# A dilated-attention merge on one Trainium2 core: weighting the other two groups' values on VectorE for all pairs of heads

## The chip, the cores and the metric

The kernel runs on one core of one Trainium2 chip (trn2). The metric is device time in microseconds; the number that counts is the median of several executions. The engines are named as in the profile: PE (TensorE, with PEld for its weight loads), DVE (VectorE), ACT (ScalarE), POOL (GpSimd), and SP, which only issues transfers. Each works through its own queue of instructions in order.

## What is computed

Two layers of an encoder, 1024 tokens of width 1024. Layer 0 mixes tokens by latent attention, layer 1 by dilated windows; each ends with a squared-ReLU MLP. The change lies in layer 1. There, 16 heads of width 64 attend in three groups of windows (window 128, 512, 2048 with dilation 1, 4, 16), and the three outputs of a head are merged by the softmax of their log denominators:

```python
DIL_GROUPS = ((128, 1), (512, 4), (2048, 16))
for gi, (window, dilation) in enumerate(DIL_GROUPS):
    q = rms_norm(proj[:, :, gi, 0], g_q[gi])
    k = rms_norm(proj[:, :, gi, 1], g_k[gi])
    o, lse = dilated_group(q, k, proj[:, :, gi, 2], pos, table, window, dilation)
...
wts = jax.nn.softmax(jnp.stack(lses, axis=0), axis=0)
o = jnp.einsum('gbsh,gbshd->bshd', wts, o_all)
y = o.reshape(B, S, DIL_HEADS * DIL_HEAD_DIM) @ w_o
```

## The kernel before

`dil` runs the three groups one after the other. In a group it goes over eight pairs of heads (`pr` 0 to 7), and a pair takes four steps (`tp` 0 to 3) of two 128-token tiles each. Work of one step is spread over several rounds of the loop, so that at any time PE has the projection of one step, the scores of the step before and the output of an earlier one.

The way of one step, with the lines by which the profile names it:

- PE projects q and k into PSUM (`psproj`, L425 to L427: most of PE's time). ACT squares (`dsq`, L1850), DVE sums (`dms`, L1851), ACT and DVE make the reciprocal root (L112 to L116), DVE scales (`qn`, L1855), POOL applies the gain (`qn`, L1857).
- PE transposes (`psq`, L1866). ACT copies the high part of the result (`kT`, L1870) and DVE writes the low part, `psq` less that copy (`kT`, L1871). PE then makes the scores (`pss`, L1891).
- DVE adds the bias and takes the maximum (`pd`, L1907), ACT exponentiates (`pd`, L1913) and rounds (`ph`, L1950), POOL subtracts (`ph`, L1951), SP starts the transposing transfer (`pT`, L1952). PE multiplies by the values (`psav`, L1964 and L1965), and DVE adds the parts into `U` (L1966).

Beside this DVE and ACT split the weights of the next pair (`wqkl` and `wqkh`, L122 and L121), and in even pairs the values of coming pairs, two tiles at a time (`vr` on DVE, L1838; `vs` on ACT and POOL, L1837, L1839, L1840).

In groups 0 and 1 `finish` writes `U` of a pair to HBM. In the third group it merges: `um` loads the two other groups' values of the same pair from HBM, issued on ACT's queue a round before, in two halves of four tiles (128 x 4 x 2 x 128 f32); `factors` makes the weights `mgf` (L2019 to L2025); `merge` multiplies `U` and the two loaded planes by their weights (L2035) and adds them (L2037). The multiplications of the loaded planes are on POOL for pairs 0 to 6 and on DVE for the last; those of `U` and the additions are on DVE. After it `emit` transposes `U` on PE (`psot`, L2054). So an even pair's merge meets the value splits on DVE and POOL and an odd pair's doesn't.

The last pair's steps run beside the first output projection (`psy`), for which DVE splits the weights `wol`. This stretch, from the merge of pair 6 on, is called the tail here.

PE's order in `dil` is pinned as written. The orders of the other engines are set by the scheduler at build time from its own costs: an instruction that moves from one engine to another shifts its neighbours too.

Of the kernel before, what the change touches and what calls it, by code (L numbers as in the profile page):

```python
# [15 lines left out]
ALU = mybir.AluOpType  # L16
# [4 lines left out]
P = 128  # L21
# [20 lines left out]
class K:  # L42
# [1717 lines left out]
    def dil(self, at0, at1, tail, wqk, vd):  # L1760


        nc, a, tc = self.nc, self.a, self.tc
# [212 lines left out]
        def finish(u):  # L1976
# [25 lines left out]
            if pr < 7:  # L2002
                f = factors(pr, 0, 8)
                for hf in range(2):
                    merge(u, hf, f[:, :, 4 * hf : 4 * hf + 4])
                merged.append((u, u["at"], (0, 1)))
            else:
                last(u, 1)
# [19 lines left out]
        def merge(u, hf, f):  # L2028
            U = u["U"][:, 4 * hf : 4 * hf + 4, :]
            x = u["um"][hf]  # L2030
            heads = lambda y: y.rearrange("p t (h e) -> p t h e", h=2)
            for k, y in ((2, U), (1, x[:, :, 1]), (0, x[:, :, 0])):
                y4 = heads(y)
                eng = nc.gpsimd if k < 2 and u["pr"] < 7 else nc.vector
                eng.tensor_tensor(y4, y4, f[:, k].unsqueeze(3).broadcast_to([P, 4, 2, 64]), op=ALU.mult)  # L2035
                if k < 2:
                    nc.vector.tensor_tensor(U, U, y, op=ALU.add)  # L2037

        def last(u, hf):

            merge(u, hf, factors(u["pr"], 4 * hf, 4))
            merged.append((u, u["at"], (hf,)))
# [97 lines left out]
        for n, step in enumerate(steps):  # L2140
# [11 lines left out]
            if step is not None:  # L2152
                kind, g, pr, tp = step
# [4 lines left out]
                u = units[(g, pr)]  # L2158
# [229 lines left out]
```

## Time and profile before

| | us |
|---|---|
| median of 3 runs (3236.93 to 3240.54) | 3239.43 |
| the profiled execution | 3241.06 |
| its span in the trace | 3239.3 |
| POOL, multiplications of the loaded planes (L2035), 28 | 35.1 |
| POOL, all instructions, from 2283 to 2497 | 112.3 |
| DVE, all instructions, from 2283 to 2497 | 179.1 |
| PE, all matmuls, from 2283 to 2497 | 205.3 |

Positions are microseconds from the start of the span. The third group's merges begin at 2286, 2320, 2353, 2387, 2421, 2456 and 2492 (pairs 0 to 6); the tail then reaches to about 2560. A row of the timeline has start, length, engine, line, operation, output and inputs, and in brackets how long the engine was idle before it and what ended that. A row of groups has the count, the sum of busy time, the mean in ns, and the idle time before. Rows of one instruction can overlap by a tenth of a microsecond or so, since the next starts while the last drains.

### The profile page before, as it was taken

What the parts mean: (1) busy time and instruction counts of PE and PEld (TensorE: products, weight loads), DVE (VectorE), ACT (ScalarE), POOL (GpSimd) and SP (SyncE); (2) the same over time, 40 slices, a digit from 0 to 9 for tenths busy, and PEclk for the clock granted to TensorE, in tenths of its full rate; (3) what the DMA queues carried; (4) which work ended last, traced back from release to release, by engine and by line L of the source; (5) the groups of instructions that cost most, each with busy time, mean ns of one, the idle gap of its engine ahead of it and who ended that gap; (6) DMA issues with size and microseconds to landing.
All of it is one profiled execution on the core that took longest, in us unless ns stands there. A gap on an engine that the chain in (4) does not pass through costs nothing. (4 is left out here: it accounts for less than half of the span.)

```text
span 3239.3 us, 50775 instructions
## 1 busy us (share of the span) xinstructions
PE 3129.4 (97%) x18034; PEld 2646.8 (82%) x18034; DVE 2380.9 (74%) x4243; ACT 1733.1 (54%) x3507; POOL 920.0 (28%) x1226
## 2 busy tenths in 40 slices
PE   6989999999999999989999999998998999999999
PEld 6877677778788788767889998998998788888887
DVE  5677778746977776688757777777788588778566
ACT  5547777754544443542226676667565264544332
POOL 7454556530111100001124444444454002110010
PEclk9999999999999999999999999999999999999999
DMA  5352322253555779544638877887777636448664
GB/s 192 121 186 82 98 94 92 63 173 111 180 199 172 269 217 316 169 150 166 227 120 180 184 172 177 192 193 159 175 166 195 180 105 209 151 151 315 202 191 128
DMA packets 538927, 552.32 MB, mean 171 GB/s; under 512 B 199429, under 2 KB 421042, under 8 KB 538666
## 3 DMA queue, kind: packets, MB, share of 16 engines
q1 hardware_dynamic: 483978, 434.61, 47.3%
q0 software_dynamic: 27360, 91.31, 7.6%
q10 hardware_dynamic: 27328, 23.07, 2.7%
q8 instruction: 144, 2.36, 0.3%
q14 instruction: 117, 0.96, 0.1%
HBM read 376.17 MB, written 132.62 MB: 157 GB/s over the span
## 5 line engine op out<-in xcount | busy, mean ns | idle before, releaser
L426 PE MATMUL psm<-dl,dh 128*128 128x512 f32 x896 | 351.0, 392 | 8.6 <-DVE dl L122 8.5
L425 PE MATMUL psm<-hf,wf 128*128 128x512 f32 x896 | 349.5, 390 | 2.6 <-ACT wf L121 2.6
L427 PE MATMUL psm<-dh,dl 128*128 128x512 f32 x896 | 350.3, 391 | 0.0
L426 PE MATMUL psm<-hf,wf 128*128 128x512 f32 x896 | 348.6, 389 | 0.0
L427 PE MATMUL psm<-hf,wf 128*128 128x512 f32 x896 | 346.6, 389 | 0.4 <-DVE wf L122 0.4
L425 PE MATMUL psm<-dh,dh 128*128 128x512 f32 x896 | 335.0, 391 | 4.0 <-ACT dh L121 4.0
L425 PE MATMUL psproj<-wqkh,hTp 128*128 128x256 f32 x1024 | 301.6, 295 | 0.0
L427 PE MATMUL psproj<-wqkh,hTp 128*128 128x256 f32 x1024 | 290.1, 283 | 0.0
L426 PE MATMUL psproj<-wqkl,hTp 128*128 128x256 f32 x1024 | 289.9, 283 | 0.1
L121 ACT ACTIVATE dh<-ufr 128x1024 fp32r<-128x1024 f32 x112 | 118.3, 1057 | 175.0 <-PE psm L427 49.7
L426 PEld LDWEIGHTS psm<-dl,dh 128*128 128x128 f32 x896 | 169.2, 189 | 46.3 <-DVE dl L122 11.3
L425 PEld LDWEIGHTS psproj<-wqkh,hTp 128*128 128x128 f32 x1024 | 196.3, 192 | 8.5 <-issue 0.4
L425 PEld LDWEIGHTS psm<-dh,dh 128*128 128x128 f32 x896 | 168.4, 188 | 41.0 <-ACT dh L121 6.3
L425 PEld LDWEIGHTS psm<-hf,wf 128*128 128x128 f32 x896 | 168.2, 188 | 40.0 <-ACT wf L121 5.5
L427 PEld LDWEIGHTS psm<-dh,dl 128*128 128x128 f32 x896 | 169.1, 189 | 35.2
L427 PEld LDWEIGHTS psm<-hf,wf 128*128 128x128 f32 x896 | 168.2, 188 | 35.9 <-DVE wf L122 1.2
L426 PEld LDWEIGHTS psproj<-wqkl,hTp 128*128 128x128 f32 x1024 | 196.5, 192 | 0.3 <-DVE wqkl L122 0.3
L426 PEld LDWEIGHTS psm<-hf,wf 128*128 128x128 f32 x896 | 168.2, 188 | 34.7
L427 PEld LDWEIGHTS psproj<-wqkh,hTp 128*128 128x128 f32 x1024 | 196.2, 192 | 0.3 <-DVE hTp L2126 0.2
L122 DVE TENSOR_TENSOR dl<-ufr,dh 128x1024 fp32r<-128x1024 f32 x112 | 136.6, 1220 | 76.8 <-ACT dh L121 58.0
L756 DVE TENSOR_REDUCE mx<-pmx 128x1 f32<-128x512 f32 x256 | 165.1, 682 | 28.2 <-PE pmx L754 28.0
L122 POOL TENSOR_TENSOR pl<-p,ph 128x1024 fp32r<-128x1024 f32 x58 | 141.4, 2439 | 138.4 <-ACT ph L121 128.2
(400 smaller groups left out, 8926.4 us busy)
## 6 DMA issues: line engine op xcount, KB each, us to landing
ufr<-uf SPq DMA_DIRECT2D x112, 512.0 KB
adaw<-in_ada_w SPq DMA_DIRECT2D x96, 512.0 KB
w2r<-in_mlp_w SPq DMA_DIRECT2D x96, 512.0 KB
w1r<-in_mlp_w SPq DMA_DIRECT2D x64, 512.0 KB
bt<-bias SPq DMA_DIRECT2D x128, 256.0 KB
qkv<-st SPq DMA_DIRECT2D x32, 512.0 KB
hraw<-qkv SPq DMA_DIRECT2D x32, 512.0 KB
uf<-ub POOLq DMA_DIRECT2D x32, 512.0 KB, 3.8
```

Source lines behind the costliest of these rows:

```text
L121: nc.scalar.activation(hi, src, AF.Copy)
L122: (lo_eng or nc.vector).tensor_tensor(lo, src, hi.bitcast(F32), op=ALU.subtract)
L425: mm(out, lh, rh, start=first, stop=False)
L426: mm(out, lh, rl, start=False, stop=False)
L427: mm(out, ll, rh, start=False, stop=last)
L756: nc.vector.tensor_reduce(maxes[h][:, 2 * j + b : 2 * j + b + 1], ps, op=ALU.max, axis=AX.X)
```

## The change

The multiplications of the two loaded planes go to DVE for every pair. The two for the last pair were there already; 28 of them move, four for each of pairs 0 to 6. Nothing else is edited, and the same numbers are computed.

```diff
             for k, y in ((2, U), (1, x[:, :, 1]), (0, x[:, :, 0])):
                 y4 = heads(y)
-                eng = nc.gpsimd if k < 2 and u["pr"] < 7 else nc.vector
-                eng.tensor_tensor(y4, y4, f[:, k].unsqueeze(3).broadcast_to([P, 4, 2, 64]), op=ALU.mult)
+                nc.vector.tensor_tensor(y4, y4, f[:, k].unsqueeze(3).broadcast_to([P, 4, 2, 64]), op=ALU.mult)
                 if k < 2:
                     nc.vector.tensor_tensor(U, U, y, op=ALU.add)
```

Lines behind it move up by one: L2035 becomes L2034, L2037 becomes L2036.

The first place is DVE's queue at the merge of pair 2, which begins at 2353.33 in the profile. `U_30939` is that pair's output, `um_31807` and `um_31810` the loaded planes of its two halves, `mgf` the weights.

```order
-L2035 TENSOR_TENSOR U_30939<-U_30939,mgf_32018 128x512
+L2034 TENSOR_TENSOR U_30939<-U_30939,mgf_32018 128x512
+L2034 TENSOR_TENSOR um_31807<-um_31807,mgf_32018 128x4x128 x2
+L2034 TENSOR_TENSOR um_31810<-um_31810,mgf_32018 128x4x128 x2
 L1966 TENSOR_REDUCE U_30939<-psav_31869 128x128
+L2036 TENSOR_TENSOR U_30939<-U_30939,um_31807 128x512
 L1966 TENSOR_REDUCE U_30939<-psav_31875 128x128
 L1851 TENSOR_REDUCE dms_31882<-dsq_31881 128x8
-L2037 TENSOR_TENSOR U_30939<-U_30939,um_31807 128x512
```

All four multiplications stand together at the head of the merge, the second half's too, before the sums of `psav` and the `dms` of the running step; in POOL's queue the four rows are gone from behind `vs` (L1840).

The second place is the same queue some fifteen instructions on, in the same round. `wqkl` are the low parts of the next pair's weights.

```order
-L122 TENSOR_TENSOR wqkl_31903<-wqkr_31757,wqkh_31902 128x1024
 L116 SCALAR_TENSOR_TENSOR dry_31885<-drt_31887,dry_31885 128x8
-L122 TENSOR_TENSOR wqkl_31907<-wqkr_31760,wqkh_31906 128x1024
 L1855 TENSOR_TENSOR qn_31893<-psproj_31813,dry_31885 128x512
 L1838 TENSOR_TENSOR vr_31897<-vraw_31489,vs_31896 128x512
+L122 TENSOR_TENSOR wqkl_31903<-wqkr_31757,wqkh_31902 128x1024
 L1871 TENSOR_TENSOR kT_31495<-psq_31973,kT_31495 128x2x256
 L1966 TENSOR_REDUCE U_30939<-psav_32004 128x128
+L122 TENSOR_TENSOR wqkl_31907<-wqkr_31760,wqkh_31906 128x1024
 L1966 TENSOR_REDUCE U_30939<-psav_32010 128x128
```

One of the two weight splits now stands behind `kT` (L1871) instead of ahead of it, and `qn` is ahead of both.

The third place is DVE's queue in the tail, from the first addition of pair 6's first half on (`U_33179`).

```order
+L2036 TENSOR_TENSOR U_33179<-U_33179,um_34033 128x512
+L122 TENSOR_TENSOR wol_34238<-wor_34235,woh_34237 128x1024
+L1871 TENSOR_TENSOR kT_33729<-psq_34192,kT_33729 128x2x256
 L114 SCALAR_TENSOR_TENSOR drt_34117<-dms_34112,dry_34115 128x8
-L2037 TENSOR_TENSOR U_33179<-U_33179,um_34033 128x512
-L115 SCALAR_TENSOR_TENSOR drt_34117<-drt_34117,dry_34115 128x8
-L122 TENSOR_TENSOR wol_34238<-wor_34235,woh_34237 128x1024
-L116 SCALAR_TENSOR_TENSOR dry_34115<-drt_34117,dry_34115 128x8
-L1871 TENSOR_TENSOR kT_33729<-psq_34192,kT_33729 128x2x256
-L1855 TENSOR_TENSOR qn_34123<-psproj_34039,dry_34115 128x512
+L2036 TENSOR_TENSOR U_33179<-U_33179,um_34033 128x512
 L1966 TENSOR_REDUCE U_33179<-psav_34241 128x128
```

Here `qn` (L1855), L115 and L116 fall behind the sums of `psav` (L1966), and the second weight split and `kT` come earlier in the sequence; the four multiplications of pair 6 stand further ahead, behind its multiplication of `U`.

PE's order in the stretch of the merges stays as it was; in the tail a few matmuls, and in the second MLP more of them and the splits that feed them, change places.

## The prediction

> **What bounds the kernel now.** I read the page's engine row first, then busy time by stage, then what PE waited for in the stage of the change, then the single waits.
>
> ```profile
> PE 3129.4 (97%) x18034; PEld 2646.8 (82%) x18034; DVE 2380.9 (74%) x4243; ACT 1733.1 (54%) x3507; POOL 920.0 (28%) x1226
> core 0: us, PE busy (x) PEld busy (x) DVE busy (x) ACT busy (x) POOL busy (x), PEclk, DMA share, GB/s
> 2283.00:2497.00 214.00, 205.28 (x1867) 196.18 (x1866) 179.11 (x503) 130.26 (x437) 112.31 (x127) 1.00 0.74 171
> 2497.00:2560.00 63.00, 53.95 (x300) 43.12 (x299) 40.70 (x103) 20.76 (x64) 2.73 (x4) 0.97 0.64 188
> ...
> PE pss L1891 <- DVE kT L1871: 4.7, 4, 1.7
> PE psav L1964 <- DMA pT<-ph: 4.0, 5, 1.5
> ...
> 2364.41 0.86 PE L1891 MATMUL pss<-kT 64*128 64x256 f32 x10 [1.58 <-DVE kT L1871]
> 2389.69 0.26 PE L1964 MATMUL psav<-vs,pT 128*128 128x192 bf16 x1 [1.47 <-DMA pT<-ph]
> 2504.46 1.65 PE L1891 MATMUL pss<-kT 64*128 64x256 f32 x12 [4.85 <-DVE U L1966]
> ```
>
> PE is the bound: 97% of the span, and 205.3 of 214 us in the stretch of the seven merges. What a change off PE can do is lengthen or shorten PE's waits, and these are few: 4.7 us for DVE's `kT`, 4.0 us for transposing transfers, then 4.85 us at the start of the tail for DVE's sums. DVE is the second engine there, 179.1 of 214 us (84%), and it gets the work. POOL, which loses it, has 112.3 and stands first in none of PE's waits.
>
> **What moves, and its price.**
>
> ```profile
> L2035 POOL TENSOR_TENSOR um<-um,mgf 128x512 f32<-128x512 f32 x28 | 35.1, 1283 | 2.4 <-PE psav L1965 2.4
> ...
> L2035 DVE TENSOR_TENSOR um<-um,mgf x4: 684/688/691, 2511.9 to 2540.7; 128x512 f32<-128x512 f32 x4
> ...
> 2511.87 1.29 DVE L2035 TENSOR_TENSOR um<-um,mgf 128x512 f32<-128x512 f32 x2
> ```
>
> POOL loses 28 multiplications, 35.1 us. The same instruction stands on DVE already for the last pair, at 0.688 us; two in a row take 1.29, so each further one takes 0.61. DVE gets 28 x 0.61 = 17.1 us, 2.44 us at each merge. Taken alone that raises DVE to 196 of 214 us.
>
> Against it stands what POOL's multiplications cost DVE. Means in the stretch, and below them least, middle and greatest length:
>
> ```profile
> L2037 DVE TENSOR_TENSOR U<-U,um 128x512 f32<-128x512 f32 x24 | 20.5, 854 | 0.3
> L2035 DVE TENSOR_TENSOR U<-U,mgf 128x512 f32<-128x512 f32 x12 | 14.6, 1213 | 0.0
> L114 DVE SCALAR_TENSOR_TENSOR drt<-dms,dry 128x8 f32<-128x8 f32 x24 | 6.4, 265 | 0.1
> ...
> L2037 DVE TENSOR_TENSOR U<-U,um x32: 681/692/1360, 2289.3 to 2548.4; 128x512 f32<-128x512 f32 x32
> L2035 DVE TENSOR_TENSOR U<-U,mgf x16: 677/952/1714, 2286.2 to 2546.9; 128x512 f32<-128x512 f32 x16
> L114 DVE SCALAR_TENSOR_TENSOR drt<-dms,dry x24: 153/161/1005, 2291.7 to 2486.7; 128x8 f32<-128x8 f32 x24
> ```
>
> DVE instructions that read two SBUF tensors are at times two or six times as long as they need. The additions lose 24 x (0.854 - 0.69) = 3.9 us, L114 24 x (0.265 - 0.16) = 2.5, the multiplications of `U` 12 x (1.213 - 0.68) = 6.4. Not all of it goes away, as the even merge shows; about 10 us should, so DVE's net gain of work is some 7 us.
>
> **An even merge (pair 2).** The walk is along DVE:
>
> ```profile
> 2353.33 1.16 POOL L1840 TENSOR_TENSOR vs<-vr,vs 128x512 bf16<-128x512 f32 x1
> 2353.33 1.71 DVE L2035 TENSOR_TENSOR U<-U,mgf 128x512 f32<-128x512 f32 x1
> 2354.45 5.40 POOL L2035 TENSOR_TENSOR um<-um,mgf 128x512 f32<-128x512 f32 x4
> 2356.49 1.00 DVE L2037 TENSOR_TENSOR U<-U,um 128x512 f32<-128x512 f32 x1
> 2358.87 1.00 DVE L114 SCALAR_TENSOR_TENSOR drt<-dms,dry 128x8 f32<-128x8 f32 x1
> 2360.01 1.23 DVE L122 TENSOR_TENSOR wqkl<-wqkr,wqkh 128x1024 fp32r<-128x1024 f32 x1
> 2361.33 1.23 DVE L122 TENSOR_TENSOR wqkl<-wqkr,wqkh 128x1024 fp32r<-128x1024 f32 x1
> 2362.47 0.68 DVE L1855 TENSOR_TENSOR qn<-psproj,dry 128x512 f32<-128x512 f32 x1
> 2363.67 0.68 DVE L1871 TENSOR_TENSOR kT<-psq,kT 128x512 fp32r<-128x512 f32 x1
> 2372.39 0.69 DVE L1851 TENSOR_REDUCE dms<-dsq 128x8 f32<-128x512 f32 x1 [0.72 <-ACT dsq L1850]
> 2379.87 0.69 DVE L1871 TENSOR_TENSOR kT<-psq,kT 128x512 fp32r<-128x512 f32 x1 [2.03 <-ACT kT L1870]
> ...
> 2380.86 0.98 PE L1891 MATMUL pss<-kT 64*128 64x256 f32 x12
> ```
>
> `U`'s multiplication begins with POOL's L1840 and ends 0.6 us after that does: L1840 held it up, and stays, so its 1.71 us stay. L114 ends when POOL's fourth multiplication does (2359.85); it gets 0.84 us shorter, the first addition 0.31. Net: 2.44 - 0.84 - 0.31 = +1.29 us. In the new order one `wqkl` (1.14 us to the next start) falls behind `kT`, so the first `kT`, for which PE waits 1.58 us, comes only 1.29 - 1.14 = 0.15 us later. But that work comes back before the next `kT`: DVE has no gap from 2353.33 until the 0.72 us before 2372.39, and goes into that step 1.29 us late. One step on, `kT` ends at 2380.56, 0.30 us before PE uses it, and ACT, which sets that one, itself hangs on DVE's earlier L1907. Bounds are 0.15 us (the gaps swallow the rest) and 1.29 us; because of the 0.30 us I take the whole, 1.3 us for each of pairs 0, 2 and 4: 3.9 us. The additions queued behind the multiplications feed `psot` a step later, which has time.
>
> **An odd merge (pair 3).**
>
> ```profile
> 2387.02 1.51 DVE L2035 TENSOR_TENSOR U<-U,mgf 128x512 f32<-128x512 f32 x1
> 2388.62 1.36 DVE L2037 TENSOR_TENSOR U<-U,um 128x512 f32<-128x512 f32 x1
> 2396.70 0.69 DVE L1871 TENSOR_TENSOR kT<-psq,kT 128x512 fp32r<-128x512 f32 x1 [0.16 <-ACT kT L1870]
> ...
> 2398.20 0.98 PE L1891 MATMUL pss<-kT 64*128 64x256 f32 x12
> ```
>
> Here POOL's own first multiplication held `U` (1.51 to 0.68) and its second the addition (1.36 to 0.69): net 2.44 - 0.83 - 0.67 = +0.94 us, against 0.81 us between the end of `kT` and PE's use. The 1.47 us wait for `pT` is a transfer's and stays. Between 0 and 0.94 I take 0.3 us for each of pairs 1, 3 and 5: 0.9 us.
>
> **The tail (pair 6).**
>
> ```profile
> 2495.38 2.08 DVE L122 TENSOR_TENSOR wol<-wor,woh 128x1024 fp32r<-128x1024 f32 x1 [2.72 <-ACT woh L121]
> 2497.38 0.68 DVE L2035 TENSOR_TENSOR U<-U,mgf 128x512 f32<-128x512 f32 x1
> 2503.30 1.01 DVE L1966 TENSOR_REDUCE U<-psav 128x128 f32<-128x384 f32 x2
> ```
>
> PE's 4.85 us end with these sums, whose PSUM banks it needs. Ahead of them now stand 2.44 us more; `wol` loses 0.85 us of POOL's hold (2.08 to 1.23); `qn` (0.60) and about 0.2 us of small ones fall behind. Net +0.8 us at PE's wait. What falls behind is late next: `qn`, and L1907 by four multiplications less 0.85, so the last transposes. Bounds 0.8 and 2.44; I take 2.0.
>
> **New waits.** The multiplications wait for `um`'s loads; on DVE the sums, `dms` and L1907 are queued behind them. POOL's multiplications waited once, and not for a load:
>
> ```profile
> POOL um L2035 <- PE psav L1965: 2.4, 1, 2.4
> ```
>
> They started with or just after `U`'s multiplication, as they will now. I cost this at nothing. So too the shuffled order in the MLP, where DVE and ACT run ahead of a PE that is always full; without that cover it is a wait of the size of those above.
>
> **Sum:** 3.9 + 0.9 + 2.0 = 6.8 us. 3241.06 + 6.8 = 3247.9 for an execution like the profiled one; the median of the runs is 1.6 us below that one, so 3246.2. I say 3246, 0.2% more than 3239.43, and 0.2% (6.5 us) is also about what a measurement of this kernel can tell from no change.
>
> **Rivals.**
>
> *Covered.* DVE's gaps swallow all but the lower bounds: 3 x 0.15 + 0.8 = 1.3 us, hence 3240.7. For it: DVE is idle 16% of the stretch, and the gaps of 0.72 and 2.03 us. Against: none lies within 18 us of an even merge's start.
>
> *Freed.* It gets faster: POOL's hold was what made DVE late at `kT`, and the scheduler's shift of a `wqkl` behind it ends those waits. Place: the four waits for `kT`, 4.7 us, and with `wol` shorter up to 2.5 of the tail's 4.85. Price -7.2 us, 3232.2. It decides if DVE loses more than 2.44 us of held time per merge; the rows give 1.15 to 1.5. [...]
>
> *Unrelieved.* Other POOL work slides into the freed time and holds DVE as before, the new multiplications included: the gross 17.1 us reach PE, 3256.5. For it: L1840 and L1951 have two inputs and stand next in POOL's queue. It decides if `L2034` on DVE runs well over 0.7 us.
>
> *Clock.* PEclk is 1.00 in the stretch of merges, where no PE wait passes 1.7 us, and 0.97 over the 63 us with the 4.85 us wait: 1.9 us lost. If even merges' waits grew that long, three would cost 3 x (3 + 1.9) = 15 us: 3254. [...]
>
> **How the numbers follow.** Forecast 0.44 (its own range 3242 to 3252, two thirds of it beyond 0.2%: 0.29), covered 0.14, freed 0.20 (0.14 of it beyond 0.2%), unrelieved 0.17, clock 0.05. Slower: 0.29 + 0.17 + 0.05 = 0.51. Faster 0.14, within 0.2% 0.35. The range runs from 3232, where freed ends, to 3257, the gross price; outside are the far ends of three cases.
>
> **What would show it.** DVE in the same stretch about 7 us busier than 179.1 and L114 near 0.16 us show the relief; PE's wait for `kT` grown from 4.7 to about 8 us, in even pairs, the forecast; the tail's first wait about 5.6 us, the third term. A `kT` wait that falls speaks for freed, `L2034` on `um` over 0.9 us for unrelieved. PE waiting for `um`'s sums, or DVE idle ahead of `um`, would make the free terms wrong.

## The result, and the profile after

The changed kernel takes 3251.16 us, the median of 7 runs (3248.64 to 3253.80), beside 3239.43 us for seven runs of the kernel before: the ratio is 1.0035, with a 95% interval from 1.0025 to 1.0044. That is 11.7 us slower. Run again later, the pair gave 3253.50 against 3240.11 us (ratio 1.0042, 1.0030 to 1.0054).

The profiled execution of the changed kernel took 3253.80 us. Its page's engine row, with busy time, share of the span and number of instructions:

```profile
PE 3134.0 (96%) x18034; PEld 2650.5 (82%) x18034; DVE 2391.9 (74%) x4271; ACT 1733.2 (53%) x3507; POOL 893.6 (27%) x1198
```

POOL lost 26.4 us of the 35.1 its multiplications had shown, and DVE gained 11. Busy time by stage of the changed kernel; the first two stretches are those shown before, the third runs from the end of PE's wait ahead of the first merge to the transposes of pair 6, so that it holds the same work as the stretch of the kernel before under it:

```profile
core 0: us, PE busy (x) PEld busy (x) DVE busy (x) ACT busy (x) POOL busy (x), PEclk, DMA share, GB/s
2283.00:2497.00 214.00, 201.05 (x1767) 191.57 (x1766) 178.75 (x509) 123.88 (x419) 82.55 (x95) 0.96 0.69 156
2497.00:2560.00 63.00, 50.91 (x323) 42.06 (x322) 41.10 (x112) 22.03 (x73) 5.33 (x7) 0.92 0.59 179
...
2266.00:2528.40 262.40, 239.77 (x2050) 226.70 (x2051) 210.47 (x608) 144.83 (x493) 91.58 (x106) 0.94 0.73 177
```

The kernel before, the stretch of the same work:

```profile
2269.20:2515.30 246.10, 230.78 (x2050) 218.37 (x2051) 201.63 (x580) 145.12 (x493) 117.08 (x134) 0.99 0.76 179
```

Read by fixed positions DVE does not seem busier (178.75 against 179.11), but the changed kernel gets through less work in 214 us: 1767 matmuls, not 1867. Over equal work, 2050 matmuls in both, DVE has 28 instructions and 8.8 us more, and the stretch is 16.3 us longer. Not all of that is waiting: PEclk fell from 0.99 to 0.94. The span as a whole is 12.7 us longer; some 3 us came back ahead of the merges, where the wait in front of them ends at 2266.0 and not at 2269.2; over the 14 profiled executions below that point lies anywhere from 2263.0 to 2271.1, so those 3 us need not be the change's.

What PE waited for between 2280 and 2500 in the changed kernel (microseconds in total, times, longest), and its longest single waits, each in the brackets behind the instruction that waited:

```profile
PE pss L1891 <- DVE kT L1871: 6.6, 3, 2.3
PE psav L1964 <- DMA pT<-ph: 5.3, 3, 2.7
PE pss L1891 <- ACT kT L1870: 0.8, 1, 0.8
```

```profile
2296.06 0.79 PE L1891 MATMUL pss<-kT 64*128 64x256 f32 x4 [2.25 <-DVE kT L1871]
2365.51 0.74 PE L1891 MATMUL pss<-kT 64*128 64x256 f32 x8 [2.07 <-DVE kT L1871]
2384.13 0.26 PE L1964 MATMUL psav<-vs,pT 128*128 128x192 bf16 x1 [2.69 <-DMA pT<-ph]
2439.35 0.58 PE L1891 MATMUL pss<-kT 64*128 64x256 f32 x2 [2.33 <-DVE kT L1871]
2466.50 0.31 PE L1964 MATMUL psav<-vs,pT 128*128 128x192 bf16 x1 [1.92 <-DMA pT<-ph]
2520.48 0.77 PE L425 MATMUL psy<-woh,oT 128*128 128x512 f32 x1 [5.39 <-issue]
```

The three even merges make PE wait 2.25, 2.07 and 2.33 us for `kT` (before 1.68, 1.58 and 1.17), two odd ones 2.69 and 1.92 us for a transposing transfer. (`issue`, in the last row, stands where the engine waited for nothing that the profile shows.)

The clock around such waits, in stretches of 14 us of the changed kernel (columns as above), and under them the first of these of the kernel before:

```profile
2290.00:2304.00 14.00, 11.75 (x93) 11.16 (x92) 13.86 (x38) 10.47 (x35) 6.90 (x6) 0.88 0.24 59
2360.00:2374.00 14.00, 11.93 (x110) 11.38 (x108) 13.86 (x38) 11.59 (x38) 7.45 (x7) 1.00 0.33 57
2382.00:2396.00 14.00, 11.01 (x77) 10.19 (x78) 7.75 (x26) 5.82 (x21) 3.37 (x5) 0.76 0.92 198
```

```profile
2290.00:2304.00 14.00, 12.32 (x110) 11.82 (x109) 13.85 (x38) 10.19 (x33) 8.37 (x9) 1.00 0.26 58
```

A wait of 1.68 us left the clock at 1.00, and so did that of 2.07 us (second row); those of 2.25 and 2.69 us were followed by 0.88 and 0.76. In the trace's record of the granted clock the changed kernel has half speed (0.5) for 3.41 us at 2295.9, 2439.3 and 2466.6, for 6.83 at 2384.7 and for 10.24 in the tail; the kernel before has it, from the first merge on, for 3.41 us in the tail alone.

So I split the stretch from the end of the wait ahead of the first merge to the first matmul of the second MLP into time in which PE waits, and time lost to half speed (half of the time at half speed in which PE does not wait; what the wait in front of the first merge leaves is not counted). The half is an estimate from the granted 0.5: in the changed kernel a 128x256 matmul (L425 to L427) starts every 0.21 us from 2297.8 to 2299.3, at half speed, and every 0.12 us from 2299.4 to 2301.1, at full speed, by which the lost share would be 0.44. Before: 17.8 and 1.6 us. After: 25.1 and 10.4. The change costs 7.3 us of waits and 8.8 us of clock in this execution.

Last, DVE's groups in the changed kernel, from 2283 to 2500 (count, sum, mean in ns, idle time before):

```profile
L122 DVE TENSOR_TENSOR wqkl<-wqkr,wqkh 128x1024 fp32r<-128x1024 f32 x12 | 18.0, 1502 | 0.0
L2034 DVE TENSOR_TENSOR um<-um,mgf 128x512 f32<-128x512 f32 x24 | 16.9, 763 | 0.0
L2036 DVE TENSOR_TENSOR U<-U,um 128x512 f32<-128x512 f32 x24 | 16.5, 687 | 0.0
L2034 DVE TENSOR_TENSOR U<-U,mgf 128x512 f32<-128x512 f32 x12 | 9.2, 767 | 0.0
L114 DVE SCALAR_TENSOR_TENSOR drt<-dms,dry 128x8 f32<-128x8 f32 x24 | 5.3, 222 | 0.2 <-ACT dry L113 0.2
```

The relief is there: additions 687 ns (854 before), `U`'s multiplications 767 (1213), L114 222 (265). The new multiplications run at 763 ns, and DVE is never idle ahead of them. But the weight splits `wqkl` got longer, 1502 ns where the kernel before (2283 to 2497) has

```profile
L122 DVE TENSOR_TENSOR wqkl<-wqkr,wqkh 128x1024 fp32r<-128x1024 f32 x12 | 14.7, 1224 | 0.1
```

so 3.3 us of the relief are lost again. At the merge of pair 2 one sees where, on DVE with one row of POOL among it:

```profile
2354.36 3.45 DVE L2034 TENSOR_TENSOR um<-um,mgf 128x512 f32<-128x512 f32 x4
...
2362.73 1.04 POOL L1857 TENSOR_TENSOR qn<-qn,dgain 128x256 f32<-128x256 f32 x1 [7.28 <-DVE qn L1855]
2363.10 1.75 DVE L122 TENSOR_TENSOR wqkl<-wqkr,wqkh 128x1024 fp32r<-128x1024 f32 x1
2364.78 0.68 DVE L1871 TENSOR_TENSOR kT<-psq,kT 128x512 fp32r<-128x512 f32 x1
```

The split that stays ahead of `kT` now runs beside POOL's L1857 and takes 1.75 us; before, both splits were done (2362.56) before POOL began L1857 (2363.30), and took 1.23 us each.

### The profile page after: what moved, and what is told of

It is laid out like the page before. It is cut to its first block, busy times and chain, and to the rows that moved or that the text cites. A ratio compares the mean times of both kernels' runs of the same rounds, so it can differ in the third digit from the quotient of the medians.

```text
span 3252.0 us, 50772 instructions
## 1 busy us (share of the span) xinstructions
PE 3134.0 (96%) x18034; PEld 2650.5 (82%) x18034; DVE 2391.9 (74%) x4271; ACT 1733.2 (53%) x3507; POOL 893.6 (27%) x1198
## 3 DMA queue, kind: packets, MB, share of 16 engines
q8 instruction: 144, 2.36, 0.3%
## 5 line engine op out<-in xcount | busy, mean ns | idle before, releaser
L425 PE MATMUL psm<-hf,wf 128*128 128x512 f32 x896 | 349.6, 390 | 2.6 <-ACT wf L121 2.6
L427 PE MATMUL psm<-dh,dl 128*128 128x512 f32 x896 | 350.7, 391 | 0.0
L427 PE MATMUL psm<-hf,wf 128*128 128x512 f32 x896 | 346.7, 389 | 0.4 <-DVE wf L122 0.4
L425 PE MATMUL psm<-dh,dh 128*128 128x512 f32 x896 | 335.3, 391 | 4.6 <-ACT dh L121 4.6
L425 PE MATMUL psproj<-wqkh,hTp 128*128 128x256 f32 x1024 | 303.9, 297 | 0.0
L427 PE MATMUL psproj<-wqkh,hTp 128*128 128x256 f32 x1024 | 291.4, 285 | 0.0
L425 PEld LDWEIGHTS psproj<-wqkh,hTp 128*128 128x128 f32 x1024 | 198.3, 194 | 8.9 <-issue 1.5
L425 PEld LDWEIGHTS psm<-dh,dh 128*128 128x128 f32 x896 | 168.4, 188 | 41.8 <-ACT dh L121 7.0
L425 PEld LDWEIGHTS psm<-hf,wf 128*128 128x128 f32 x896 | 168.2, 188 | 40.1 <-ACT wf L121 5.5
L427 PEld LDWEIGHTS psm<-dh,dl 128*128 128x128 f32 x896 | 169.6, 189 | 35.3
L427 PEld LDWEIGHTS psproj<-wqkh,hTp 128*128 128x128 f32 x1024 | 198.1, 193 | 0.2 <-DVE hTp L2125 0.2
L427 PEld LDWEIGHTS psm<-hf,wf 128*128 128x128 f32 x896 | 168.2, 188 | 35.9 <-DVE wf L122 1.1
L1857 POOL TENSOR_TENSOR qn<-qn,dgain 128x256 f32<-128x256 f32 x96 | 92.0, 958 | 350.2 <-DVE qn L1855 312.0
```

The source lines that it names most:

```text
L425: mm(out, lh, rh, start=first, stop=False)
L427: mm(out, ll, rh, start=False, stop=last)
L1857: nc.gpsimd.tensor_tensor(qq, qq, gain[:, g : g + 1, :].unsqueeze(1).broadcast_to([P, 2, 2, 64]), op=ALU.mult)
```

## The experiments

Theory A, after the result: the four multiplications at the head of a merge make `kT` late, PE waits longer, and waits of about 2 us also cost clock. Rival B: the scheduler's other order of ACT's work and of the loads does it. Rival C: it is the tail. All kernels ran beside the kernel before on the same chip, in three groups. Waits and half-speed time are worked out for one profiled execution of each, as above; they differ by some microseconds from one execution to the next, the medians less. The ratio is estimated from all runs and is not the quotient of the two medians (pair 6 alone: 0.9996 and 0.9989).

| kernel | median, and before's beside it, us | ratio, 95% interval | PE waits, us | lost at half speed, us |
|---|---|---|---|---|
| before | 3239.43 | | 17.8 | 1.6 |
| changed | 3251.16, 3239.43 | 1.0035, 1.0025 to 1.0044 | 25.1 | 10.4 |
| changed, again | 3253.50, 3240.11 | 1.0042, 1.0030 to 1.0054 | 22.3 | 9.0 |
| even pairs | 3248.47, 3241.03 | 1.0028, 1.0016 to 1.0039 | 23.1 | 10.1 |
| odd pairs | 3240.89, 3241.03 | 1.0005, 0.9993 to 1.0017 | 18.6 | 4.7 |
| pair 6 alone | 3238.73, 3242.25 | 0.9996, 0.9987 to 1.0005 | 16.1 | 8.3 |
| left out | 3240.31, 3241.03 | 0.9998, 0.9987 to 1.0010 | 16.3 | 3.4 |
| late | 3236.67, 3241.03 | 0.9990, 0.9979 to 1.0002 | 16.2 | 1.7 |
| late, again | 3239.09, 3240.11 | 0.9999, 0.9990 to 1.0007 | 15.9 | 5.1 |
| halves | 3252.78, 3242.25 | 1.0038, 1.0026 to 1.0051 | 23.9 | 7.0 |
| halves, late | 3249.94, 3240.11 | 1.0030, 1.0020 to 1.0040 | 24.8 | 9.4 |
| order of loads | 3243.69, 3242.25 | 1.0000, 0.9990 to 1.0010 | 17.4 | 4.1 |
| twice | 3262.12, 3242.25 | 1.0061, 1.0048 to 1.0075 | 32.1 | 9.6 |
| filled | 3260.72, 3240.11 | 1.0067, 1.0053 to 1.0081 | 22.7 | 13.6 |

PE's waits part the kernels that are slower than the kernel before (22.3 us and more) from those that can't be told from it (18.6 us and less). The loss at half speed of a single execution does so less well: 7.0 us and more against 1.6 to 8.3, and the 1.6 us of the kernel before, from which the 8.8 us above are counted, is the least of all.

**Even pairs alone, and odd pairs alone.**

```diff
-                nc.vector.tensor_tensor(y4, y4, f[:, k].unsqueeze(3).broadcast_to([P, 4, 2, 64]), op=ALU.mult)
+                eng = nc.gpsimd if k < 2 and u["pr"] in (1, 3, 5, 6) else nc.vector
+                eng.tensor_tensor(y4, y4, f[:, k].unsqueeze(3).broadcast_to([P, 4, 2, 64]), op=ALU.mult)
```

Odd pairs: the same with `(0, 2, 4, 6)`.

> The planes' multiplications are on VectorE in the even pairs 0, 2 and 4 alone; pairs 1, 3, 5 and 6 keep them on GpSimd. Theory A (VectorE's extra work at a merge makes kT late, PE waits longer, and waits of about 2 us also cost granted clock): the kT waits of pairs 0, 2 and 4 stay at 2.1 to 2.3 us as in the changed kernel, the pT waits of the odd pairs fall back to 1.5 us or less; 3 to 6 us over the kernel before, 3242 to 3245. Rival B (the loss is the other order of loads and of ACT's work in the odd pairs, whose pT waits grew to 1.9 and 2.7 us): within 2 us of before. Rival C (the loss is in the tail alone): also within 2 us of before.

> The planes' multiplications are on VectorE in the odd pairs 1, 3 and 5 alone; pairs 0, 2, 4 and 6 keep them on GpSimd. Theory A: VectorE has 0.8 us to spare in an odd pair, so kT waits grow little and the time is at most 3 us over before (3239 to 3242). Rival B: the pT waits of pairs 3 and 5 are 1.9 to 2.7 us as in the changed kernel, each with a dip of the granted clock, and the time is 4 to 8 us over before (3243 to 3247). Rival C: within 2 us of before.

Even pairs: ratio 1.0028, 9 us by the ratio and 7.4 between the medians, more than the 3 to 6 that A expected; odd pairs not to be told from before. PE's waits between 2280 and 2500 with the even pairs alone:

```profile
PE pss L1891 <- DVE kT L1871: 7.2, 4, 2.4
PE psav L1964 <- DMA pT<-ph: 6.2, 4, 2.0
```

The waits for `kT` are the changed kernel's (2.31, 2.36 and 2.35 us at the three even merges). But A was wrong in one point: the transfer waits of the odd pairs did not fall back, though their multiplications are on POOL again.

**The multiplications left out.** The planes of pairs 0 to 6 are added without their weights.

```diff
-                nc.vector.tensor_tensor(y4, y4, f[:, k].unsqueeze(3).broadcast_to([P, 4, 2, 64]), op=ALU.mult)
+                if k == 2 or u["pr"] == 7:
+                    nc.vector.tensor_tensor(y4, y4, f[:, k].unsqueeze(3).broadcast_to([P, 4, 2, 64]), op=ALU.mult)
```

> The planes of pairs 0 to 6 are added without being weighted: 28 multiplications are left out of both engines. This gives the relief without its price. If GpSimd's hold on VectorE was part of what made kT late: kT waits fall from 4.7 us to 1 to 2 us, and the time is 3 to 6 us under before (3233 to 3236). If the hold never mattered to PE: within 2 us of before. If the order of ACT's work and of the loads is what costs, and that order moves with any change of the merge: 3 us or more over before.

Nothing gained: 0.9998. PE still waits at the merge of pair 2, once for ACT's half of `kT` and once for DVE's:

```profile
2363.46 0.45 PE L1891 MATMUL pss<-kT 64*128 64x256 f32 x2 [0.77 <-ACT kT L1870]
2365.03 0.57 PE L1891 MATMUL pss<-kT 64*128 64x256 f32 x2 [1.11 <-DVE kT L1871]
```

Together 1.88 us, where the kernel before waited 1.58. So taking the multiplications away altogether gained nothing that these runs can tell. At pair 2 the relief did not reach `kT`: both `wqkl` are still ahead of it and take 1.77 and 1.63 us instead of 1.23 each.

**Late.** All 28 on DVE, but those of a pair's second half held behind the second half's multiplication of `U`, a step later.

```diff
+            bb, lead = self.nc.cur_bb.bb.instructions, None
             for k, y in ((2, U), (1, x[:, :, 1]), (0, x[:, :, 0])):
...
+                if k == 2:
+                    lead = bb[-1]
+                elif hf and u["pr"] < 7:
+                    self.tc.add_manual_dep(bb[-1], lead.name, mybir.DependencyInfo(
+                        mybir.DependencyClass.NoSync, mybir.DependencyReason.DATA), reason="late")
```

> All on VectorE as in the changed kernel, but the two multiplications of a pair's second half stand behind the second half's multiplication of U, a step later: two and not four at the head of a merge. Theory A: the first kT of an even merge is 1.2 us earlier than in the changed kernel, its waits fall under 1.5 us, with no dip of the clock there; 2 to 7 us over before (3241 to 3246), so 5 to 10 us under the changed kernel. Rivals B and C, for which the place of the work does not matter: as the changed kernel, 3249 to 3253.

Better than A expected: 0.9990, no slower than before, and 0.9999 when run again. DVE at the merge of pair 2:

```profile
2350.87 1.28 DVE L2035 TENSOR_TENSOR um<-um,mgf 128x512 f32<-128x512 f32 x2
...
2359.13 0.68 DVE L1871 TENSOR_TENSOR kT<-psq,kT 128x512 fp32r<-128x512 f32 x1
...
2363.83 1.28 DVE L2035 TENSOR_TENSOR um<-um,mgf 128x512 f32<-128x512 f32 x2
```

Two multiplications stand ahead of `kT` and two behind it. From the start of `U`'s multiplication to the start of `kT` DVE takes 9.8 to 9.9 us at the three even merges; in the kernel before it is 10.3 to 10.4, in the changed one 11.0 to 11.1. The waits for `kT` there are 1.12, 0 and 0.90 us, and over the same 2050 matmuls the clock does not fall:

```profile
2264.70:2509.40 244.70, 230.41 (x2050) 216.90 (x2051) 206.66 (x605) 144.32 (x493) 86.71 (x106) 1.00 0.80 183
```

DVE still has 5.0 us more work than before, and the stretch is 1.4 us shorter. So at the even merges it is not the amount on DVE that costs, but how late `kT` comes behind the head of the merge, and for that how much stands in one piece ahead of it. The late kernel is not free of waits: a transfer's of 1.85 us stands ahead of pair 2's merge, and its second execution has three of 2.1 to 2.4 us and loses 5.1 us at half speed.

**Halves.** The first half's multiplications on POOL, the second half's on DVE, where the scheduler puts them at the head of the merge.

```diff
-                eng = nc.gpsimd if k < 2 and u["pr"] < 7 else nc.vector
+                eng = nc.gpsimd if k < 2 and u["pr"] < 7 and hf == 0 else nc.vector
                 eng.tensor_tensor(y4, y4, f[:, k].unsqueeze(3).broadcast_to([P, 4, 2, 64]), op=ALU.mult)
```

> The planes' multiplications of a pair's second half are on VectorE, those of the first half on GpSimd, for pairs 0 to 6: 14 of 28 move, all of them at the head of a merge; the order of the loads on ScalarE's queue stays as in the kernel before. Theory A (work at the head of a merge makes kT late, and from waits of about 2 us on the granted clock falls too): even kT waits of about 2 us, some with a dip; 2 to 6 us over before. Rival B (in the changed kernel the loads' other order costs, by later transposing transfers in the odd pairs): within 2 us of before.

With 14 of 28 moved it is as slow as the whole change, more than the 2 to 6 us that A expected, and the order of the loads is that of before, so B can't be the cause here. DVE, then POOL, then PE at the merge of pair 2:

```profile
2354.60 2.98 DVE L2035 TENSOR_TENSOR um<-um,mgf 128x512 f32<-128x512 f32 x2
...
2361.36 1.23 DVE L122 TENSOR_TENSOR wqkl<-wqkr,wqkh 128x1024 fp32r<-128x1024 f32 x1
...
2362.68 1.23 DVE L122 TENSOR_TENSOR wqkl<-wqkr,wqkh 128x1024 fp32r<-128x1024 f32 x1
```

```profile
2354.09 2.94 POOL L2035 TENSOR_TENSOR um<-um,mgf 128x512 f32<-128x512 f32 x2
```

```profile
2364.54 0.46 PE L1891 MATMUL pss<-kT 64*128 64x256 f32 x2 [2.55 <-DVE qn L1855]
2366.23 0.39 PE L1891 MATMUL pss<-kT 64*128 64x256 f32 x2 [1.23 <-DVE kT L1871]
```

Two multiplications on each engine at the same time take 2.94 to 2.98 us on both, where two on DVE alone take 1.28; and both `wqkl` stay ahead of `qn` and `kT`. From the start of `U`'s multiplication to `kT` it is 12.5 us, and PE waits 3.78 us, more than with all four on DVE.

**Halves, late.** The same 14 on DVE, held as in the late kernel: the edits of the last two together.

> The same 14 multiplications on VectorE and the same 14 on GpSimd as in the halves on two engines, but VectorE's stand behind the second half's multiplication of U, a step later, instead of at the head of the merge. If the place on VectorE's queue is what costs: at least 6 us less than that kernel's +11 to +12, so between 3 us under and 5 us over before, even kT waits back to 1.7 us or less. If the amount on VectorE and GpSimd's hold on it are what costs: as that kernel, 9 us or more over before.

PE's waits for DVE's `kT` fell to 1.1 us in all between 2280 and 2500, as the place on the queue would have it. Yet the whole is 1.0030, 9.8 us over before, and so not what was expected of the place: three transfer waits of 5.07, 5.12 and 3.08 us stand in the odd pairs. This led to the second mechanism. In the round ahead of an odd merge ACT issues the next pair's weights (`wqkr`, L1562) just as SP issues the transposing transfer of one step. The kernel before, this kernel and the changed one, the rows of the loads' first issue, of the transfer and of who waits for it:

```profile
2372.33 1.23 SPq L1952 DMA_TRANSPOSE pT<-ph  x1
...
2372.58 0.39 ACTq L1562 DMA_DIRECT2D wqkr<-in_dil_w_in  x1
```

```profile
2376.10 0.38 ACTq L1562 DMA_DIRECT2D wqkr<-in_dil_w_in  x1
...
2378.58 1.82 SPq L1952 DMA_TRANSPOSE pT<-ph  x1
...
2389.12 0.34 PE L1964 MATMUL psav<-vs,pT 128*128 128x192 bf16 x1 [5.12 <-DMA pT<-ph]
```

```profile
2373.65 0.38 ACTq L1562 DMA_DIRECT2D wqkr<-in_dil_w_in  x1
...
2374.90 1.23 SPq L1952 DMA_TRANSPOSE pT<-ph  x1
...
2384.76 0.42 ACT L1950 ACTIVATE ph<-pd 128x256 f16<-128x256 f32 x1 [4.10 <-DMA pT<-ph]
```

Before, the transfer is 0.25 us ahead of the first load and is there in time, within 7.9 us. Here it is 2.48 us behind and takes 10.5; in the changed kernel, at this merge, 1.25 us behind and 9.2, and ACT's next L1950 waits for it too, 4.10 us. The 14 profiled executions have three such meetings each: in 34 the transfer was issued first, and PE waited for it in none; in 8 (three each in this and the filled kernel, one in the even pairs' and one in the changed) it came second, and PE waited 1.25 to 5.12 us in all 8. The changed kernel's second execution has none: between the transposes of pairs 2 and 3 it waits 1.6 us and loses nothing at half speed, where the first waits 3.6 and loses 3.0. The order was seen, not set by an edit of its own. Nor is it shown that the loads slow the transfer: the eight took 7.7 to 10.5 us, and where one took 7.7 (filled) its late issue alone explains the wait.

**Order of loads.** The kernel before, with the last load of weights held behind L1911 and `um`'s loads behind L1913 in the odd pairs, as ACT's queue has them in the changed kernel.

```diff
+                    if u["pr"] in (1, 3, 5):
+                        self.behind(old[1])
...
+            old = getattr(self, "mark1", None), getattr(self, "mark2", None)
             transposed, scored = scored, attend(ready, n > end) if ready else []
+            if getattr(self, "put", None):
+                self.put()
+                self.behind(old[0])
+                self.put = None
```

> The kernel before (GpSimd multiplies), with only the order on ScalarE's queue ahead of the odd merges made that of the changed kernel: the last load of weights stands behind L1911, the first load of um behind L1913. Rival B: the pT waits of the odd pairs grow to 1.5 to 2.7 us, with dips of the clock, and the time is 3 to 8 us over before. Theory A: pT waits as before (1.5 us or less), within 2 us of before.

1.0000: B falls for these later loads. (Its transfers went out ahead of the first load, by 0.23 us.)

**Pair 6 alone.** The condition is `u["pr"] < 6` in the edit of the halves, for both halves.

> On VectorE for pair 6 alone, the one in front of the tail; pairs 0 to 5 keep GpSimd. By the prediction's tail term: +2.0 us (0.8 to 2.4), PE's first long wait of the tail about 5.6 us. By the profile of the changed kernel: waits of the stretch of pair 6 from 7.6 to 9.7 us, +2.1 us, and with the longer time of low clock there +2.9. If even, odd and tail pairs add up to the whole (7.4 for even, about 0 for odd, 10 to 12 for all): 2.5 to 4.5 us.

PE's first long wait of the tail is what the prediction had, 5.6 us:

```profile
2509.24 0.58 PE L1891 MATMUL pss<-kT 64*128 64x256 f32 x2 [5.56 <-DVE U L1966]
```

But the two shorter ones behind it (1.54 and 0.20 us before) are gone, waits up to pair 6's transposes are 5.8 us, not 7.6, and the time is not longer. By the ratios, even, odd and this one add up to 1.0028 + 0.0005 - 0.0004 = 1.0029, 9.4 us; by the medians they add up to 3.8 us. The whole is 11.7, so these runs don't show whether the three parts are all of it.

**Twice.** Each of the 28 multiplications done twice, so that the output is weighted twice there.

```diff
+                if k < 2 and u["pr"] < 7:
+                    nc.vector.tensor_tensor(y4, y4, f[:, k].unsqueeze(3).broadcast_to([P, 4, 2, 64]), op=ALU.mult)
```

> The changed kernel with each of the 28 moved multiplications done twice on VectorE (the output is weighted twice there): 17.1 us of further work. Theory A: no slack is left at the even merges, nearly all of it reaches PE as waits and the clock falls behind each of them: 17 to 30 us over the changed kernel, 3268 to 3281. Rival, VectorE's gaps take it (it is idle 16% of the stretch): 0 to 6 us over the changed kernel.

Both missed: 1.0061 against the changed kernel's 1.0035 to 1.0042, so 6 to 8 us for 17.1 us of work. All eight multiplications stand ahead of `kT` at an even merge, but the scheduler put `qn`, `vr` and one addition behind it, so that `kT` starts 10.6 us behind `U`'s multiplication. What fell behind is late in its turn: `qn` makes PE wait at every merge. The odd merges now wait too, for `qn`, which both engines handle:

```profile
2414.05 0.41 PE L1866 MATMUL psq<-ident,qn 128*128 128x128 f32 x2 [1.99 <-DVE qn L1855]
2415.14 0.41 PE L1866 MATMUL psq<-ident,qn 128*128 128x128 f32 x1 [0.68 <-POOL qn L1857]
```

**Filled.** The changed kernel with 20 transposes of the unit matrix on PE ahead of the scores that wait for `kT`.

```diff
-            q = u["q"].pop(t)
+            q = u["q"].pop(t); fill(nc, u, t, pss, self.ident)
...
+    if u["g"] == 2 and u["pr"] % 2 and t == 2:
+        for _ in range(20):
+            nc.tensor.transpose(pss[0][:, 256:384], ident, ident)
```

> The changed kernel with work for TensorE that has no use: 20 transposes of the unit matrix, by the rate of psq's some 1.75 us, ahead of the scores of the second step of pairs 1, 3, 5 and 7, where the long kT waits stand; their output is overwritten. The scheduler moves some of VectorE's and ScalarE's work around them. If waits of 2 us and more also cost granted clock: these waits fall to about 0.5 us, the dips behind them go, and the kernel is 2 to 6 us faster than the changed one in spite of the further work. If only the waits cost: the filling takes their place, as the changed kernel within 1 us, or slower by up to 7 us where it delays what waits on TensorE.

The whole is 7 us slower than the changed kernel, not faster. At the even merges it did what A says. PE there, and then at the odd merge behind it:

```profile
2366.62 2.35 PE L2393 MATMUL pss<-ident 128*128 128x128 f32 x20
2368.90 1.30 PE L1891 MATMUL pss<-kT 64*128 64x256 f32 x12
```

```profile
2386.55 0.26 PE L1964 MATMUL psav<-vs,pT 128*128 128x192 bf16 x1 [1.25 <-DMA pT<-ph]
2389.41 0.65 PE L1891 MATMUL pss<-kT 64*128 64x256 f32 x2 [2.14 <-ACT kT L1870]
```

No wait, no fall of the clock, and the stretches from one pair's transposes to the next with the merges of pairs 2 and 4 in them took 34.9 and 35.3 us, against 36.7 and 36.4 in the changed kernel on the same chip, although PE did 2.3 us of useless work in each. That work fills the wait of 2.3 us that was there; the 1.8 and 1.1 us gained are near the 1.7 us that each of these stretches lost at half speed. But the scheduler moved DVE's and ACT's work around it, the transfers fell 1.37 us behind the loads in all three odd pairs, and these stretches took 39.2 to 39.8 us instead of 33.1 to 35.9. So the clock's part is shown at two places, and the whole time says nothing on it.

**The changed kernel and the late one again.**

> The changed kernel unedited, beside the others of this call on one chip: 8 to 14 us over before, the granted clock some 0.002 under before's.

> The late kernel a second time, on another day of the chip or another chip: if its gain is real, 1 to 6 us under before again; if it was chance, within 2 us of before or over it.

The loss repeats (1.0042). The late kernel's gain does not: 0.9999, within 0.2% of before both times. No version tried is faster than the kernel before beyond doubt.

The granted clock of every run, and not of one execution, says where the loss lies. On the chip of the last group the changed kernel's six runs have a mean clock of 0.9857, the kernel before's twenty 0.9889; time by one less the clock is 46.6 and 36.1 us. So 10.5 of the 13.0 us between the means go with the lower clock (the half of waits at half speed among it), and 2.5 are left. The same count gives 3.9 of 11.2 us for the halves and 2.9 of 20.2 for twice: the clock is not the larger part in every kernel.

## Why the prediction came out as it did

The sign was right, and 3251.2 lies in the range; the forecast of 3246 was 5 us short, and its own range of 3242 to 3252 barely held; the repeat, 3253.5, lies above it.

- **The sum of waits, 6.8 us,** came near: 7.3 us in one execution, 4.5 in the other. In part that is luck, since two terms missed in opposite directions.
- **Even merges, 3 x 1.3:** the right pairs, too large, and at another `kT`. The three waits grew by 2.2 us in all, by 2.6 in the second execution, so some 0.8 us each, and this at the first `kT`, which was to come 0.15 us later. It came 0.6 to 0.7 us later behind the merge's head, because the split that stays ahead of it takes 1.75 us, not 1.23. The next `kT`, for which the 1.3 us were taken, made PE wait at one of the six even merges of the two executions, 0.79 us for ACT's half behind a late transfer. DVE's net work was near, 8.8 us more where some 7 were forecast.
- **Odd merges, 3 x 0.3:** too small, and the wrong wait. `kT` was not late at all: one split fell behind it here too, and it follows `U`'s multiplication by 8.1 to 9.4 us where before it took 9.6 or 9.7. But PE's transfer waits, of which the prediction said they stay, grew by 3.4 us (with `kT`'s wait on ACT behind one of them) and by 1.6. One reason was seen above: what comes late from a merge falls behind a burst of loads, with a quarter of a microsecond to spare. The waits of about 2 us at the third odd merge, and why they stand in the even pairs' kernel, are not settled; the order of loads and pair 6 alone have one each (2.08 and 2.01 us) without being slower.
- **The tail, 2.0:** its waits did grow by 2.1 and 0.9 us, but not at the forecast place: the wait for the sums, 4.85 us before and forecast at 5.6, is gone in the changed kernel, and 5.39 us stand ahead of the output projection. The wait of 5.6 us came with pair 6 alone, which, at most 1.6 us by its interval, does not cost 2.0.
- **New waits and the MLP, 0:** right. DVE is idle 0.0 us ahead of `um`, and from the second MLP's first matmul to the end of the last one it is 619.74 us, 619.73 before.
- **Freed** fell: without any multiplication nothing was gained. **Unrelieved** fell as a price, 17.1 us, and by its sign: L2034 runs at 0.76 us, not over 0.9. But what it says happened in part, on another instruction: POOL's other work holds the splits `wqkl`, 3.3 us over the twelve, and the one ahead of `kT` gives 0.5 of the 0.7 us by which `kT` is late at pair 2.
- **The clock** is the step that failed. As a rival it had 0.05, since I took a wait of 4.85 us as what it needs, the only one in the stretch with a fall behind it. In the runs waits of 2.2 us or more nearly always do (35 of 37), and that is what even merges reached. Its mechanism was right: by the count over all runs 10.5 of 13.0 us go with the clock, and in the two executions half speed takes 8.8 and 7.4 us more than in the one of the kernel before. Its condition, waits of 4.85 us at the even merges, never came, so that its 3254 lies nearer to the result than 3246 is luck. The sum itself put the clock at nothing.

Behind the sum lay a wrong picture: that DVE's net work counts. The late kernel has all 28 multiplications and 5.0 us of net work, and costs nothing.

## What to carry to other kernels

When work moves to an engine that feeds the bound one, ask how much of it lands in one piece ahead of the next thing that the bound engine waits for, and split it there before costing the sum. Look for waits that are already near the length behind which the clock fell here (in 35 of 37 cases at 2.2 us or more): 0.6 to 1.2 us more of waiting at an even merge cost up to 1.7 us more here. Where a late result goes out by DMA, compare its issue with the next burst on the other queue; a margin of 0.25 us is little, and in 8 of 42 cases here the order turned. And ask what the engine that is relieved does next: its other work can hold the same neighbour, as the split `wqkl` on DVE took 1.75 us beside POOL's L1857 here, and 1.23 without it.

## What the runs showed of the hardware

- Half speed came in pieces of 3.41, 6.83 or 10.24 us. Over the stage of the 14 profiled executions, with waits less than 2.5 us apart added up: behind 28 waits of 0.9 to 1.6 us it came never, behind 40 of 1.67 to 2.17 us in 13, behind 37 of 2.2 us or more in 35.
- Two multiplications of 128x512 by `mgf` took DVE 1.28 us where POOL did none of them (late, 2350.87 and 2363.83); with POOL doing two of the same beside it (halves, at the merge of pair 2), they took 2.98 us on DVE and 2.94 on POOL.
